# A DiT block on one Trainium2 core: the stream of the modulation rows and router weights moves from the last rank to the second

## The chip, the cores and the metric

The kernel is written in Bass for one core of a Trainium2 chip. The metric is the device time of one execution in microseconds (us). The engines are PE (TensorE: matmuls; PEld are its weight loads), DVE (VectorE), ACT (ScalarE), POOL (GpSimd) and SP (SyncE, which issues nearly all transfers, one after the other, in the order of its queue).

## What is computed

One layer over 1024 latent tokens of width 1024, with 256 context tokens ahead of them. Eight RWKV heads (a bidirectional recurrence) and four attention heads work on the same normalised input; their outputs, 512 columns each, are put side by side and go through one 1024x1024 output projection, scaled by a gate. Then each token is routed to 4 of 32 experts.

```python
p_lat = modulate(rmsnorm(x, norm1_g[l]), sh1, sc1) @ w_in[l]
y_rwkv, yc_rwkv = rwkv_mixer(p_lat[..., :RWKV_COLS], ...)
y_mla, yc_mla = mla_mixer(p_lat[..., RWKV_COLS:], ...)
x = x + gt1 * (jnp.concatenate([y_rwkv, y_mla], axis=-1) @ w_out[l])
h2 = modulate(rmsnorm(x, norm2_g[l]), sh2, sc2).reshape(B * T, D)
f = moe_ffn(h2, router_w[l], router_b[l], exp_w1[l], exp_b1[l], exp_w2[l], exp_b2[l])
x = x + gt2 * f.reshape(B, T, D)
return rmsnorm(x, final_norm_g)
```

The change touches the line with `w_out`: `gt1` (the gate) must be spread to all 128 partitions before it can be multiplied into `w_out`, and the scale and shift rows of the second modulation and the router's weights must be there before the logits of the router.

## The kernel before

The program has two phases. The first, some 1290 of 2711 us, is the mixer: projections, recurrence, attention, output projection and routing. The second, the 32 experts, is written in a fixed order and is not touched.

**The planner.** The mixer is not written in the order in which it runs. Each piece of work is a Python generator, a *stream*, which yields the engine, buffer or event that it wants next. A planner (`Weave`) keeps an estimated clock for each engine and lets, among the streams that its estimate holds ready for the engine that is free first, the one with the lowest *rank* record its next step; among equals the older one. `w.spawn(rank, generator)` starts a stream. The estimates only set the order of instructions on each engine's queue; on the chip an engine runs its queue in that order and waits by semaphores. All instructions of the mixer are recorded through one helper and show as line 972, so streams are told apart by shape, tile and position.

**The streams that matter here, with their ranks:**
- rank 0: the scan of the recurrence (chunk steps 0 to 19 one after the other; four context steps, then 16 latent ones), the solver of its chunk systems, `Mix.weights`; rank 1: the feeder of the scan's operands, routing of a block;
- rank 40 to 47: `Mix.rows(m)`, the second half of the output projection of token block m (of 8), which needs the recurrence's output (k = 0 to 3 of `w_out`), `early(m)`, and all of `w_out`;
- rank 52 to 59: `Mix.early(m)`, the first half, with attention's output (k = 4 to 7): x and y are fetched, 24 matmuls 128x512 in two halves of 12, two adds, one store to `x2`;
- rank 60: `Rwkv.readout(b)`, group normalisation and gate of the recurrence's output of block b, stored as `y`; rank 61: norm and logits of a block; rank 100 and 101: what hangs on the scan's outputs;
- rank 105, the last of all: `Mix.tables`, below.

The blocks go in the order 4, 3, 5, 2, 6, 1, 7, 0, as forward and backward scan meet in the middle.

**`Mix.tables`** starts when the fifth chunk system is solved. It loads the router's weights, adds and multiplies them with the modulation (8 matmuls 128x32, DVE), and spreads the gate, scale and shift rows over the partitions: six groups of four matmuls `kc,modc` 128x128, each followed by one ACT copy. Then it fires `placed`. **`Mix.weights`** waits for the end of attention and for `placed`. It loads `w_out` in eight slices of 512 KB into three stage buffers, slices 4 to 7 first; each is multiplied with the gate row (DVE for even, POOL for odd slices), copied as the high part by ACT, and the low part is taken by a DVE subtraction 128x1024, which frees the stage buffer. After four slices `early` may run, after eight `rows`.

**What holds readouts apart.** A readout needs the one buffer `SQ` twice: for the squares early in its chain, and for the transposed result that the store to `y` reads. So the next readout's squares wait until that store has landed. The chain of one readout is squares (ACT), sum and inverse root (15 or so small DVE operations), two POOL operations, a gate matmul, a DVE product, four transposes (PE), a copy (ACT), the store (SP).

**After the last block** a short routing part (`Route.lead`) turns the logits of block 0 into slots, gathers the first expert's rows from `h_d` by POOL, transposes them, and the experts start.

Of the kernel before, what the change touches and what calls it, by code (L numbers as in the profile page):

```python
# [651 lines left out]
class Route:  # L652
# [10 lines left out]
    def start(self, jobs):  # L663
        w, ex = self.w, self.ex
        ex.begin(jobs)
        self.J = jobs[0]
        w.spawn(50, self.early())
        w.spawn(50, self.loads())
        w.spawn(70, self.conversions())
# [307 lines left out]
class Weave:  # L977
# [75 lines left out]
    def run(self):  # L1053
        while self.live:
            self.settle()
            if not self.live:
                break
            start = {}
            for s in self.live:
                if isinstance(s["need"], str):  # L1060
                    e = s["need"]
                    s["from"] = s["ready"]
                    if s["room"]:
                        s["from"] = max(s["ready"], min((x[0] for x in s["room"].free), default=1e18))
                    start[e] = min(start.get(e, 1e18), max(s["from"], self.free[e]))
            if min(start.values(), default=1e18) > 1e17:
                raise RuntimeError("streams stuck: " + str([(s["rank"], s["gen"].__name__) for s in self.live]))
            e = min(start, key=start.get)
            t = start[e]
            cool = e == "pe" and self.clock.cool(t)  # L1070
            s = min((s for s in self.live if s["need"] == e and s["from"] <= t),
                    key=lambda s: (cool and not s["dense"], s["rank"], s["no"]))
            self.began, self.now, self.lag = t, t, self.LAG[e]
            if s["room"]:
                s["send"] = self.take(s["room"])
            self.resume(s)
            s["late"] = self.now + self.lag
            s["ready"] = self.now if s["on"] or e == "sp" else s["late"]
        return self.now
# [831 lines left out]
class Attention:  # L1911
# [19 lines left out]
    def split(self, hi, lo, src):  # L1931
# [4 lines left out]
        w.dve.tensor_sub(lo, src, hi.bitcast(F32))  # L1936

    def run(self, order, start):
        w, d = self.w, self.d
        yield start  # L1940
# [588 lines left out]
class Mix:  # L2529
# [23 lines left out]
    def start(self, order):  # L2553
        w = self.w
        w.spawn(0, self.weights())
        w.spawn(105, self.tables())
        w.spawn(61, self.more())
        for i, m in enumerate(order):
            w.spawn(52 + i, self.early(m))
            w.spawn(40 + i, self.rows(m))  # L2560
# [371 lines left out]
```

## Time and profile before

| | us |
|---|---|
| median of 3 runs | 2704.86 (2703.42 to 2709.39) |
| the profiled execution | 2712.86, span 2710.9 |
| attention's last store | 977.92 |
| loads of `w_out` issued | 1045.22 to 1083.12 |
| end of the scan's last matmuls | 1096.96 |
| first rows of the experts gathered (wait begins) | 1256.43 |
| experts | about 1290 to 2710 |

Times of events are counted from the start of the span. The stretch that the change concerns lies between 920 and 1290 us. The page's shares are averages over the whole span, of which the experts are more than half, and say little about it; the stretches of time and the chain of waits of that part say more. In the table of stretches a busy time next to the length of the stretch shows how full an engine is, and PEclk is the granted clock of TensorE as a share of its full speed.

### The profile page before, as it was taken

The numbers are of one execution on the slowest core, as the hardware profiler recorded it, in microseconds if no ns is written. First come the engines' busy times: TensorE is split into PE (matmuls) and PEld (weight loads), VectorE is DVE, ScalarE is ACT, GpSimd is POOL, SyncE is SP. The second block draws the span as 40 slices with busy tenths as digits, with TensorE's granted clock in tenths as the row PEclk, the third lists the DMA queues.
The fourth block names the chain that finished last, engine by engine and source line by source line (L and its number), as shares of the span: only waits on it lengthen the run. The fifth ranks groups of instructions, "written<-read, shape, count | busy, mean of one in ns | idle before, by whom it ended". The sixth has DMA issues, their size and how long they took to land.

```text
span 2710.9 us, 58835 instructions
## 1 busy us (share of the span) xinstructions
PE 2497.3 (92%) x23393; PEld 2185.5 (81%) x23428; DVE 2035.9 (75%) x4060; ACT 1634.4 (60%) x2633; POOL 491.3 (18%) x431
## 2 busy tenths in 40 slices
PE   5999995899999998796999999999999999999996
PEld 2666763677777787565999999999999999999995
DVE  6753865777775647676887887898988888898886
ACT  6233544656545434233686776787777777777785
POOL 1112443310111136310111110111101110111101
PEclk8899997889899888897999999999999999999997
DMA  6642445552323235655798897998999989999994
GB/s 249 236 182 59 117 111 121 121 165 81 120 87 103 71 115 152 220 204 191 277 333 280 305 330 277 322 337 295 333 312 328 335 309 325 317 329 330 315 331 162
DMA packets 240985, 622.52 MB, mean 230 GB/s; under 512 B 73080, under 2 KB 157176, under 8 KB 190400
## 3 DMA queue, kind: packets, MB, share of 16 engines
q1 hardware_dynamic: 229808, 581.96, 62.3%
q0 software_dynamic: 10896, 36.74, 5.6%
q8 instruction: 186, 3.05, 0.4%
q14 instruction: 95, 0.78, 0.1%
HBM read 544.09 MB, written 74.53 MB: 228 GB/s over the span
## 4 chain that ended last, share of the span: by engine, by line
PE 61%; DVE 24%; ACT 5%; issue 3%; DMA 3%; SPq 2%; POOL 1%; DVEq 0%; ACTq 0%; POOLq 0%
PE banks L972 28%; PE banks L384 15%; DVE at L357 9%; DVE at L972 8%; PE banks L395 8%; PE banks L388 7%; ACT at L972 2%; DVE at L410 2%; SPq L972 2%; PE banks L327 1%; DVE at L411 1%; DMA at<-y_d 1%; ACT at L349 1%; ACT at L409 1%; DVE at L412 1%
## 5 line engine op out<-in xcount | busy, mean ns | idle before, releaser
L972 PE MATMUL banks<-at,at 128*128 128x512 f32 (+8 forms) x3775 | 743.1, 354 | 78.1 <-ACT at L972 31.0
L384 PE MATMUL banks<-at,at 128*128 128x256 f32 (+11 forms) x5120 | 750.7, 299 | 0.8 <-DVE at L410 0.8
L357 DVE TENSOR_TENSOR at<-at,at 128x2048 bf16<-128x2048 f32 x316 | 721.4, 2283 | 0.0
L384 PEld LDWEIGHTS banks<-at,at 128*128 128x128 f32 x5120 | 685.0, 189 | 2.5 <-DVE at L410 1.2
L972 PEld LDWEIGHTS banks<-at,at 128*128 128x128 f32 (+3 forms) x3290 | 444.5, 186 | 223.6 <-issue 74.7
L349 ACT ACTIVATE at<-at 128x2048 fp32r<-128x2048 f32 x316 | 603.5, 1910 | 0.0
L972 ACT ACTIVATE at<-banks 128x512 f32<-128x512 f32 (+6 forms) x475 | 240.3, 524 | 320.8 <-PE banks L972 308.2
L388 PE MATMUL banks<-at,at 128*128 128x128 bf16 (+11 forms) x5120 | 382.5, 226 | 0.0
L972 DVE TENSOR_TENSOR at<-at,at 128x1024 fp32r<-128x1024 f32 (+26 forms) x364 | 261.7, 728 | 112.8 <-ACT at L972 103.1
L388 PEld LDWEIGHTS <-at 128*128 128x128 bf16 x5120 | 322.8, 96 | 21.8 <-issue 3.5
L972 ACT ACTIVATE at<-at 128x512 f32<-128x512 f32 (+9 forms) x259 | 175.1, 701 | 248.3 <-DVE at L972 100.9
L395 PE MATMUL banks<-at,at 128*128 128x128 f32 (+11 forms) x2048 | 273.0, 290 | 11.7 <-DVE at L419 11.3
L409 ACT ACTIVATE at<-banks,at 128x128 f32<-128x128 f32 (+11 forms) x512 | 183.4, 375 | 157.0 <-PE banks L388 121.6
L395 PEld LDWEIGHTS banks<-at,at 128*128 128x128 f32 x2048 | 256.5, 192 | 18.6 <-DVE at L419 18.0
L972 PE MATMUL banks<-at 64*64 64x64 f32 (+4 forms) x4880 | 230.9, 231 | 41.6 <-DVE at L972 23.4
L972 PEld LDWEIGHTS banks<-at 64*64 64x64 f32 (+3 forms) x4880 | 203.5, 142 | 72.0 <-DVE at L972 31.8
L972 PE MATMUL banks<-kc,at 128*128 128x128 f32 (+4 forms) x1136 | 179.1, 288 | 38.9 <-ACT at L972 19.7
L972 POOL TENSOR_TENSOR at<-at,at 128x512 f32<-128x512 f32 (+6 forms) x106 | 149.1, 1413 | 352.6 <-DVE at L972 317.7
L313 POOL DMA_INDIRECT at<-h_d,at x49 | 47.5, 969 | 897.3 <-DVE at L295 444.2
L972 POOL TENSOR_TENSOR at<-at 64x512 f32<-64x512 f32 (+3 forms) x94 | 123.8, 1324 | 428.8 <-ACT at L972 201.0
L972 PEld LDWEIGHTS banks<-kc,at 128*128 128x128 f32 (+2 forms) x1136 | 140.3, 169 | 72.2 <-issue 29.4
L458 POOL DMA_INDIRECT x_d<-at,at x50 | 122.8, 2456 | 327.8 <-ACT at L409 150.3
(158 smaller groups left out, 2127.3 us busy)
## 6 DMA issues: line engine op xcount, KB each, us to landing
at<-in_wexp SPq DMA_DIRECT2D x384, 1024.0 KB, 7.1
at<-in_mod_w SPq DMA_DIRECT2D x48, 512.0 KB, 6.2
at<-w_d SPq DMA_DIRECT2D x48, 384.0 KB, 4.0
at<-w_d SPq DMA_DIRECT2D x32, 512.0 KB, 5.1
at<-in_w_in SPq DMA_DIRECT2D x18, 512.0 KB, 3.5
x_d<-at SPq DMA_DIRECT2D x18, 512.0 KB, 3.0
at<-in_x SPq DMA_DIRECT2D x16, 512.0 KB, 5.5
w_d<-at SPq DMA_DIRECT2D x16, 512.0 KB, 4.3
```

Source lines behind the costliest of these rows:

```text
L313: nc.gpsimd.indirect_dma_start(out=xg[:R], out_offset=None, in_=self.d["h2"], in_offset=bass.IndirectOffsetOnAxis(ap=gi[:R, 0:1], axis=0))
L327: nc.tensor.transpose(p[:, k, :R], xg[:R, kk * 128:kk * 128 + 128], ident[:R, :R])
L349: self.nc.scalar.activation(wh, J["w", s], AF.Copy)
L357: self.nc.vector.tensor_sub(wl, J.pop(("w", s)), wh.bitcast(F32))
L384: nc.tensor.matmul(p[:, q, :2 * N], wh[:, k, q], X[:, k].rearrange("p s n -> p (s n)"), start=k == 0, stop=False, skip_group_check=True)
L388: nc.tensor.matmul(p[:, q, N:2 * N], wl[:, k, q], xt[:, k, 0, :, 1], start=False, stop=k == KT - 1, skip_group_check=True)
L395: nc.tensor.matmul(p[:, q, :N], w[:, k, q], J["H"][:, k], start=k == 0, stop=k == KT - 1, skip_group_check=True)
L409: nc.scalar.activation(u[:, q], p[:, q, N:2 * N], AF.Identity, bias=b)
L410: nc.vector.tensor_add(u, p[:, :, :N], u)
L411: nc.vector.tensor_scalar(u[:, 0], u[:, 0], 7.0, None, op0=OP.min)
L458: self.nc.gpsimd.indirect_dma_start(out=self.d["x2"], in_=J["yo", i][:R], in_offset=None, compute_op=OP.add, out_offset=bass.IndirectOffse ...
L972: return f(*args, **kw)
```

## The change

One number: the rank with which `Mix.tables` is started.

```diff
     def start(self, order):
         w = self.w
         w.spawn(0, self.weights())
-        w.spawn(105, self.tables())
+        w.spawn(1, self.tables())
         w.spawn(61, self.more())
```

No operation is added or removed; the planner records the mixer in another order. Three places follow.

SP around the loads of `w_out` before (at170 to at172 are the three stage buffers; `o_d` the scan's outputs, here those of scan step 16; at132 to at134 with `w_d` and `v_d` the feeder's loads for a scan step; at146, at149 a readout's; at173, at153 with `in_x` and `y_d` those of `early`):

```order
L972 DMA at141_228<-o_d_68 128x512
L972 DMA at170_257<-in_w_out 128x1024
L972 DMA at171_258<-in_w_out 128x1024
L972 DMA at172_259<-in_w_out 128x1024
L972 DMA at146_233<-v_d_60 128x4x64 x2
L972 DMA at149_236<-xg_d_61 128x128
L972 DMA y_d_67<-at147_234 128x4x128
L972 DMA at170_257<-in_w_out 128x1024
```

And now, where the `o_d` rows are those of scan step 12:

```order
L972 DMA at140_227<-o_d_68 128x512
L972 DMA at170_257<-in_w_out 128x1024
L972 DMA at171_258<-in_w_out 128x1024
L972 DMA at172_259<-in_w_out 128x1024
L972 DMA at141_228<-o_d_68 128x512
L972 DMA at133_220<-w_d_59 128x4x256 x2
L972 DMA at133_220<-v_d_60 64x256 x4
L972 DMA at170_257<-in_w_out 128x1024
L972 DMA at171_258<-in_w_out 128x1024
L972 DMA at172_259<-in_w_out 128x1024
L972 DMA at146_233<-v_d_60 128x4x64 x2
```

The loads stand four scan steps earlier; the fourth to sixth, which wait for a stage buffer to be freed, now stand ahead of the next readout's loads and of a feeder load for the scan. The conversions follow in scan steps 13 to 15 (before: 17 to 19).

PE at the end of the scan before (64x64 are matmuls of the recurrence; the last row with at133 is the scan's last set; at158 to at161 are the high parts of `w_out` slices 4 to 7, so the rows with them belong to `early`):

```order
L972 MATMUL banks_77<-at133_220 64x64 x16
L972 MATMUL banks_77<-at148_235,at149_236 128x512
L972 MATMUL banks_77<-at138_225,at135_222 64x64 x16
L972 MATMUL banks_77<-at133_220 64x64 x16
L972 MATMUL banks_77<-kc,at145_232 128x128 x4
L972 MATMUL banks_77<-kc,at140_227 128x128 x4
L972 MATMUL banks_77<-at133_220 64x64 x16
L972 MATMUL banks_77<-at158_245,at174_261 128x512
L972 MATMUL banks_77<-at159_246,at174_261 128x512
```

The same place now (at154 to at157 are the high parts of slices 0 to 3, so the rows with them belong to `rows`):

```order
L972 MATMUL banks_77<-at133_220 64x64 x16
L972 MATMUL banks_77<-at138_225,at135_222 64x64 x16
L972 LDWEIGHTS at180_9265
L972 MATMUL banks_77<-at162_249,at180_9265 128x512
...
L972 MATMUL banks_77<-at154_241,at178_8998 128x512
L972 MATMUL banks_77<-at155_242,at178_8998 128x512
L972 MATMUL banks_77<-at156_243,at178_8998 128x512
L972 MATMUL banks_77<-at157_244,at178_8998 128x512
L972 MATMUL banks_77<-at133_220 64x64 x16
```

Before, the first of the eight `early` blocks comes behind the scan's last matmuls. Now all eight stand ahead of them (blocks 4 and 3 after step 15, two more in each of steps 16, 17 and 18), and with them block 4 of `rows` with its logits, half of block 5 and four matmuls of block 2. Behind the scan stand blocks 5, 2, 3, 6 of `rows`, then 1, 7, 0.

SP at the end of the mixer before, from readout 0's store on (at147 is the buffer `SQ`, so `y_d<-at147` is a readout's store; a fetch of `x2_d` and `y_d` begins a block of `rows`):

```order
L972 DMA y_d_67<-at147_234 128x4x128
L972 DMA h2_d_70<-at134_221 128x1024
L972 DMA x2_d_69<-at132_219 128x1024
L972 DMA at235_9175<-in_wexp 128x2048
L972 DMA at236_9176<-in_wexp 128x2048
L972 DMA at134_221<-x2_d_69 128x1024
L972 DMA at134_221<-y_d_67 128x4x128
```

And now, from readout 7's store to the fetch of block 0:

```order
L972 DMA y_d_67<-at147_234 128x4x128
L972 DMA at173_260<-x2_d_69 128x1024
L972 DMA at153_240<-y_d_67 128x4x128
L972 DMA h2_d_70<-at134_221 128x1024
L972 DMA x2_d_69<-at173_260 128x1024
L972 DMA y_d_67<-at147_234 128x4x128
L972 DMA at132_219<-x2_d_69 128x1024
L972 DMA at132_219<-y_d_67 128x4x128
L972 DMA at235_9523<-in_wexp 128x2048
```

Each of the last three blocks of `rows` (1, 7, 0) is now fetched directly behind the store of its own readout, and the two expert weights come behind the last fetch, no longer ahead of it.

## Rows read from the trace of the kernel before

**Rows 1.** Stretches (start:end, length), busy us of PE, PEld, DVE, ACT, POOL; PEclk, DMA

```profile
978.00:1002.00 24.00, 23.84 (x417) 21.34 (x418) 11.03 (x19) 8.45 (x14) 8.47 (x12) 1.00 0.50 150
1002.00:1027.00 25.00, 21.99 (x243) 18.75 (x244) 12.85 (x33) 8.70 (x15) 13.46 (x14) 0.73 0.32 87
1050.00:1073.00 23.00, 16.70 (x308) 14.12 (x306) 19.12 (x25) 12.25 (x20) 20.46 (x13) 0.94 0.41 127
1073.00:1097.00 24.00, 13.57 (x211) 10.68 (x212) 21.25 (x21) 8.04 (x12) 17.52 (x12) 0.70 0.49 151
1175.00:1200.00 25.00, 23.89 (x133) 17.63 (x136) 21.37 (x68) 8.05 (x21) 5.79 (x6) 1.00 0.67 224
978.00:1097.00 119.00, 98.57 (x1513) 84.98 (x1514) 81.24 (x132) 43.79 (x70) 70.18 (x63) 0.87 0.48 145
1097.00:1264.00 167.00, 132.65 (x698) 94.23 (x710) 108.74 (x361) 44.98 (x123) 25.30 (x31) 0.89 0.60 206
1290.00:2710.00 1420.00, 1377.34 (x13403) 1335.82 (x13401) 1196.51 (x2386) 1058.29 (x1600) 180.29 (x107) 0.99 0.88 309
```

**Rows 2.** Timeline, the scan's end: start us, us, engine, line, operation, out<-in

```profile
986.10 1.05 SPq L972 DMA_DIRECT2D at<-o_d  x2
...
1045.22 1.38 SPq L972 DMA_DIRECT2D at<-in_w_out  x3
...
1060.25 9.60 SPq L972 DMA_DIRECT2D at<-in_w_out  x3
...
1085.34 0.33 SPq L972 DMA_DIRECT2D at<-in_x  x1
...
1095.81 1.15 PE L972 MATMUL banks<-at 128*64 128x64 f32 x32
```

**Rows 3.** The chain of waits after the scan: start us, us, what

```profile
1108.99 12.10 DMA at<-y_d
...
1175.07 7.56 PE banks L972 x32
...
1219.43 11.37 DMA at<-y_d
1230.88 0.64 ACT at L972
...
1256.43 6.35 DMA at<-h_d,at
```

**Rows 4.** Timeline of PE, logits of one half block

```profile
1150.82 0.98 PE L972 MATMUL banks<-at,at 128*128 128x32 f32 x8
...
1151.63 0.63 PE L972 MATMUL banks<-kc,at 128*128 128x128 f32 x4
```

**Rows 5.** Timeline of two readouts, from squares to store (in brackets the idle time before)

```profile
1023.62 0.63 ACT L972 ACTIVATE at<-at 128x512 f32<-128x512 f32 x1
...
1036.77 0.37 SPq L972 DMA_DIRECT2D y_d<-at  x1
...
1095.65 0.37 SPq L972 DMA_DIRECT2D y_d<-at  x1
...
1098.01 0.63 ACT L972 ACTIVATE at<-at 128x512 f32<-128x512 f32 x1 [0.87 <-DMA y_d<-at]
...
1120.32 1.15 SPq L972 DMA_DIRECT2D y_d<-at  x1
```

**Rows 6.** The page's transfers: issues, KB each, median us from issue to landing

```profile
at<-in_x SPq DMA_DIRECT2D x16, 512.0 KB, 5.5
```

**Rows 7.** Timeline of POOL and DVE, conversions of `w_out` slices

```profile
1054.91 3.24 POOL L972 TENSOR_TENSOR at<-at,at 128x1024 f32<-128x1024 f32 x1
...
1058.31 3.90 DVE L972 TENSOR_TENSOR at<-at,at 128x1024 bf16<-128x1024 f32 x2
...
1064.08 2.36 POOL L972 TENSOR_TENSOR at<-at,at 128x1024 f32<-128x1024 f32 x1 [0.75 <-DMA at<-in_w_out]
1064.28 5.23 DVE L972 TENSOR_TENSOR at<-at,at 128x1024 bf16<-128x1024 f32 x2
```

## The prediction

> **What bounds the kernel now.** I read the table of stretches first, then the chain of waits behind the scan, then the timeline around single waits. The experts keep PE busy for 1377.34 of 1420 us [rows 1] in an order that the change leaves alone, and they start when the last block is routed. So the question is only when the gather of the first expert's rows begins, 1256.43 us now [rows 3]; whatever moves that moves the end by as much. Ahead of it lie two parts. Up to 1096.96 us, where the scan's last matmuls end (1095.81 + 1.15) [rows 2], the scan's serial chain sets the pace and PE works beside it for 98.57 of 119 us [rows 1]; idle are 0.2 us of the slice 978 to 1002, 3.0 of 1002 to 1027, and 6.3 and 10.4 in the two from 1050 to 1097 [rows 1]. In those last two DVE is at 19.12 of 23 and 21.25 of 24 us, since the conversions of `w_out` fall there, and the scan's own DVE steps queue behind them. Behind the scan, 159.4 us (1256.4 − 1097.0) hold all sixteen half blocks of the output projection, and PE is nearly full while there is work for it (23.89 of 25 us) [rows 1].
>
> **What moves, term by term.** Nothing is removed. The tables end before the conversions need them, the loads of `w_out` follow the `o_d` loads that stand at 986.1 instead of 1045.2 us [rows 2], and so 59 us earlier the gate is open; work of PE that lay behind the scan is now in front of its end.
>
> *PE work moved ahead of the scan's end.* An `early` block is 24 matmuls; 32 of this size took 7.56 us, 0.236 each [rows 3], so a block is 5.67 us and eight are 45.4. With them go 24 + 12 + 4 = 40 matmuls of `rows`, 9.4 us, and the logits of one block, two halves of 0.98 + 0.63 us [rows 4], 3.2 us. Sum 58.0 us.
>
> *The scan's end.* Between 978 us and the scan's end PE then has 98.6 + 58.0 = 156.6 us of work, 37.6 more than the 119 us that it had. That is what it costs if PE never idles. But the conversions now lie in steps 13 to 15 and hold DVE there, while `early` is not yet allowed to fill the gap: I move the two slices' hole of 6.3 + 10.4 = 16.7 us with them. Against that stands the clock: in the slices at a granted clock of 0.73 and 0.70 lie 21.99 and 13.57 us of PE work [rows 1]; at 1.00 these would be 16.1 and 9.5, so 10.0 us less at the most. The denser stretches in the table have 1.00, the ones with holes have not; I take half, 5 us. The scan's end goes out by 37.6 + 16.7 − 5 = +49.3 us. Bounds: +27.6 (no hole, whole clock gain) and +54.3 (hole, no gain); with DVE stalls beyond these, see the third rival.
>
> *From the scan's end to the store of readout 1.* Behind the scan PE had 132.65 us [rows 1]; without the eight `early` blocks 87.2 remain, 10.9 for each of eight blocks with norm, logits, routing and readout. Blocks 5, 2, 3 and 6 are 43.6, less 16 matmuls (3.8) done before: 39.8. At the share of the fullest stretch here, 23.89 of 25 [rows 1], that is 41.6, and one fetch that nothing covers is 5.5 us [rows 6]: 47. Bounds 42 and 52.
>
> *The last readouts.* This is where the cover goes. Now readouts 1, 7 and 0 run while PE is busy with `early` and `rows`, and all their stores are out before their blocks are due. Afterwards nothing else is left to do, and each waits for the one before, since squares need the buffer that the store reads. From squares to store a readout took 13.15 us (1023.62 to 1036.77), from a store to the next squares 2.36 us (1095.65 to 1098.01), and beside block work 22.3 (1098.01 to 1120.32) [rows 5]. On PE's queue 12 matmuls of a block stand in the middle of each (2.8 us, and they wait for a fetch): I take 13.15 + 2.36 + 4 = 19.5 us a readout, between 15.5 and 24.7, the measured pairs. After readout 1 come two: 39.
>
> *The last block.* Store landing 2.4 us [rows 5], fetch 5.5 [rows 6]: 7.9 us, where before the last fetch took 11.37 [rows 3] behind two expert loads that now come after it. From its ACT copy to the gather it was 1256.43 − 1230.88 = 25.5 us [rows 3], a chain that the change leaves alone. 39 + 7.9 + 25.5 = 72.4; bounds 64 and 88.
>
> *Sum.* 49.3 + 47 + 72.4 = 168.7 us against 159.4 behind today's scan end: +9.3 us. The profiled execution took 2712.86 us, span 2710.9, and so goes to 2722; the median of the runs, 8 us lower, from 2704.86 to 2714. The change wins 159.4 − 119.4 = 40 us behind the scan and pays 49.3 in front of its end; it is a gain only if the scan's end moves by less than 40 us.
>
> **The rivals.** *Faster: PE is not as full in the scan as it looks.* Weight loads fill only 84.98 of the 119 us against 98.57 for matmuls [rows 1], and small sets whose ends overlap may make room for `early` without holding the scan. If the hole is filled as well and the clock stays at its higher level, 2.4 GHz, the scan's end moves by +27.6 us; the tail at 114 (42 + 72) gives 27.6 + 114 − 159.4 = −17.8, 2687 us; with a part of the hole, 2692. It decides from the 40 us above. For it speaks also that the 12.10 us fetch behind the expert weights at 1108.99 [rows 3] lay open and is gone in the new order; against it, that the slice 978 to 1002 has PE at 23.84 of 24 us. The Trainium skill (Perfetto Trace Analysis, section Identifying the Most-Contended Engine) says that busy time of matmuls is a bad measure of headroom and that weight-load busy time should be used. By it the stretch has 34 us of room in place of 20, and the whole change would be a gain. The trace so far doesn't settle it: in the experts both measures stand above 0.94.
>
> *No difference.* The serial readouts run at 15.5 us, as PE has nothing else: the tail is 8 us shorter, the sum +1.3, 2706 us.
>
> *Slower still: SP and DVE stall the scan.* The fourth to sixth load of `w_out` wait on SP until a stage buffer is free; before, SP stood 9.60 us over such three loads (1060.25) and the first of them came 15.0 us after the first load (1045.22) [rows 2]. Now a feeder load of the scan and a readout's loads stand right behind. If the feeder's lead of about a step doesn't cover it, the scan waits up to 15 us: +24.3, 2729 us. The conversions may also get slower: the two subtractions without POOL beside them took 3.90 us, two with a POOL product beside them 5.23 [rows 7], 0.67 us more each, some 5 us over eight. The Trainium skill (SBUF, section Who interferes with whom) gives the reason: a DVE operation with two SBUF inputs and a GpSimd operation that reads SBUF share one port pair, an exclusive lock. The rows agree with it, and it adds nothing to the sum, as the same pairs met before.
>
> That the change does nothing is out: the queues of the engines differ from scan step 12 on, as the pieces above show.
>
> **How the numbers follow.** Forecast 0.48 (own range 2706 to 2724: 0.34 slower, 0.14 within); faster 0.24 (0.20, and 0.04 within); no difference 0.14 (0.10 within, 0.02 on either side); slower still 0.14. A measurement of this kernel can't tell 0.2 %, 5.4 us, from no change. So faster 0.22, same 0.28, slower 0.50. Range: from the middle of the faster rival to the far end of the slower one, 2690 to 2734.
>
> **What would show it.** In the profile after, the first loads of `w_out` at some 987 us; PE over 0.9 busy from about 1040 us to a scan end near 1146 us; then the stores of readouts 1, 7 and 0 some 19 us apart with PE half idle between them; a gather near 1266 us; the experts as long as before. I am wrong if the scan ends before 1130 us, if the last readouts are done under block work, or if `w_d` and `v_d` loads land late and the scan stands still in steps 13 to 15.

## The result and the profile after

The change makes the kernel slower. The median of 11 runs is 2733.38 us (2723.27 to 2739.32) against 2709.39 us (2698.13 to 2721.07) for 11 runs of the kernel before; the ratio is 1.0093, with a 95% interval of 1.0076 to 1.0109, that is +24.0 us (20.6 to 29.5 from the ends of the interval). The prediction said +9.3 us with the right sign and about the right two halves; the time lies in its range, near the far end.

The profiled execution took 2738.96 us, with a span of 2737.1. The table of stretches of the kernel after (columns as in [rows 1]) has the stretches of [rows 1] from 1002 to 1097, then the longer road to the scan's end, what lies behind it, and the experts:

```profile
1002.00:1027.00 25.00, 19.69 (x268) 17.74 (x265) 21.79 (x22) 10.65 (x14) 16.66 (x11) 0.74 0.70 217
1027.00:1050.00 23.00, 16.36 (x168) 12.28 (x168) 18.51 (x30) 6.25 (x9) 15.92 (x15) 0.70 0.53 173
1050.00:1073.00 23.00, 22.26 (x223) 16.60 (x223) 10.50 (x25) 6.10 (x10) 5.67 (x5) 1.00 0.63 181
1073.00:1097.00 24.00, 23.61 (x281) 18.39 (x284) 13.96 (x31) 5.73 (x10) 8.52 (x9) 1.00 0.68 215
1097.00:1125.00 28.00, 27.20 (x269) 20.05 (x271) 16.31 (x35) 7.79 (x15) 9.18 (x8) 1.00 0.46 144
1125.00:1160.00 35.00, 31.35 (x281) 23.75 (x284) 18.91 (x41) 9.55 (x18) 10.31 (x13) 0.85 0.49 160
...
1160.00:1210.00 50.00, 42.30 (x238) 30.61 (x242) 37.91 (x140) 16.17 (x52) 8.40 (x8) 0.83 0.48 165
1210.00:1260.00 50.00, 31.25 (x138) 21.89 (x139) 33.01 (x113) 14.12 (x38) 11.89 (x11) 0.74 0.44 144
...
1315.00:2736.00 1421.00, 1377.13 (x13405) 1335.86 (x13404) 1197.38 (x2386) 1058.36 (x1600) 176.73 (x107) 0.99 0.88 309
```

Three things are to be seen. The experts take what they took, 1377.13 us of PE against 1377.34 in [rows 1], so all of the loss is ahead of them. From 1050 to 1125 us PE is full (22.26 of 23, 23.61 of 24, 27.20 of 28) where it had holes before; the conversions, which keep DVE and POOL busy, now lie in the two slices from 1002 to 1050. And from 1210 to 1260 us PE works 31.25 of 50 us. The last 71.6 us up to the gather, in the kernel before:

```profile
1184.80:1256.40 71.60, 58.54 (x326) 42.92 (x328) 52.06 (x193) 25.48 (x74) 6.80 (x10) 0.87 0.56 194
```

and in the kernel after, where PE does 15.0 us less in the same length and its granted clock is lower:

```profile
1210.30:1281.90 71.60, 43.57 (x203) 30.56 (x205) 43.90 (x155) 17.80 (x52) 12.15 (x12) 0.73 0.44 150
```

The timeline of the kernel after, at the places of [rows 2] and [rows 5] (start us, us, engine, line, operation): the ACT operation with which scan step 12 and then step 15 starts, loads of `w_out`, the scan's last matmuls, and the last three stores of a readout, of blocks 1, 7 and 0.

```profile
981.64 0.60 ACT L972 ACTIVATE at<-banks 128x512 f32<-128x512 f32 x1
...
999.04 1.72 SPq L972 DMA_DIRECT2D at<-in_w_out  x3
...
1010.28 0.35 SPq L972 DMA_DIRECT2D at<-in_w_out  x1
...
1030.77 0.58 ACT L972 ACTIVATE at<-banks 128x512 f32<-128x512 f32 x1
...
1157.92 1.54 PE L972 MATMUL banks<-at 128*64 128x64 f32 x32
...
1210.34 0.38 SPq L972 DMA_DIRECT2D y_d<-at  x1
...
1230.11 0.43 SPq L972 DMA_DIRECT2D y_d<-at  x1
...
1251.08 0.39 SPq L972 DMA_DIRECT2D y_d<-at  x1
```

The scan's last matmuls end at 1159.46 instead of 1096.96 us, and the last three readouts store 19.8 and 21.0 us apart. The last store goes out 30.9 us ahead of the gather; before it was 44.7 us ahead, and the row of the kernel before is:

```profile
1211.73 0.37 SPq L972 DMA_DIRECT2D y_d<-at  x1
```

The chain of waits of the kernel after (start us, us, what) at the end, to be laid beside [rows 3]:

```profile
1213.71 4.67 DMA at<-y_d
...
1259.40 0.62 ACT at L972
...
1281.93 6.56 DMA at<-h_d,at
```

The gather is waited for from 1281.93 instead of 1256.43 us. The one fetch that shows takes 4.67 us, where fetches of 12.10 and 11.37 us stood before: the change did remove those, and lost more elsewhere. What took their place is in the shares of that chain from the scan's end to the gather, some 162 us before and 125 after. Before:

```profile
by line: PE banks L972 45.1%; DVE at L972 25.1%; DMA at<-y_d 14.5%; ACT at L972 5.3%; issue 4.5%; DMA at<-h_d,at 3.9%; DMA x_d<-at 2.1%; SPq L972 1.8%; DVE lg L972 0.5%; DVEq L972 0.1%; ACTq L972 0.1%
```

After:

```profile
by line: DVE at L972 46.1%; PE banks L972 32.5%; ACT at L972 9.4%; DMA at<-h_d,at 5.2%; issue 5.1%; DMA at<-y_d 3.7%; DVE lg L972 0.9%; SPq L972 0.5%; DVEq L972 0.1%; ACTq L972 0.1%
```

Fetches fall from 14.5% to 3.7%, and DVE rises from 25.1% to 46.1%, that is from some 41 to 58 us: the small operations of norms, routing and readouts, which ran beside block work before, now are links of the chain.

**One execution is not one instruction's time.** Step 12 of the scan, in which the loads of `w_out` now go out, starts at 974.52 us in the profile of before and at 981.64 in that of after. Over the 17 profiles of this study it starts between 969.1 and 982.1 us, in no order that goes with the change: the two kernels of the study that keep `tables` at its old rank and move a readout's rank have 970.8 and 970.7, the change measured again 970.6. So those 7.1 us are for the most part spread between executions (what the tables' own work may have of them stands further down), and from here on the stretch from step 12 to the gather is compared, cut at the scan's end (the end of the DVE copy 64x512 of step 19, 1.2 to 1.7 us ahead of the last matmuls' end). "Idle" is the length less PE's busy time. All in us, one profiled execution each.

| kernel | step 12 to scan's end | PE idle | scan's end to gather | PE idle | step 12 to gather | scan's end to last readout store | last store to gather |
|---|---|---|---|---|---|---|---|
| before | 120.8 | 20.4 | 161.2 | 27.8 | 281.9 | 116.5 | 44.7 |
| before, again (e9) | 119.6 | 19.7 | 160.9 | 27.7 | 280.5 | 116.0 | 44.9 |
| after | 176.6 | 19.0 | 123.7 | 36.1 | 300.3 | 92.8 | 30.9 |
| after, again (e8) | 176.8 | 16.5 | 125.7 | 35.1 | 302.5 | 94.8 | 30.9 |

The two pairs differ by 18.4 and 22.0 us, 20 in the mean; the rest of the 24.0 us of the medians was not located. Single profiles carry an error of their own: that of e10 below is 8.2 us short of the median of its kernel (2710.17 and 2718.39 us), so a few us between two stretches say nothing.

### The profile page after: what moved, and what is told of

It is laid out like the page before. It is cut to its first block, busy times and chain, and to the rows that moved or that the text cites. A ratio compares the mean times of both kernels' runs of the same rounds, so it can differ in the third digit from the quotient of the medians.

```text
span 2737.1 us, 58807 instructions
## 1 busy us (share of the span) xinstructions
PE 2519.3 (92%) x23388; PEld 2200.8 (80%) x23428; DVE 2034.8 (74%) x4060; ACT 1633.8 (60%) x2633; POOL 488.3 (18%) x431
## 4 chain that ended last, share of the span: by engine, by line
PE 62%; DVE 25%; ACT 5%; issue 3%; DMA 3%; SPq 2%; POOL 1%; DVEq 0%; ACTq 0%; POOLq 0%
PE banks L972 29%; PE banks L384 15%; DVE at L972 9%; DVE at L357 9%; PE banks L395 8%; PE banks L388 7%; ACT at L972 2%; DVE at L410 2%; SPq L972 1%; PE banks L327 1%; DVE at L411 1%; ACT at L409 1%; DVE at L412 1%; ACT at L349 1%; PE banks L452 1%
## 5 line engine op out<-in xcount | busy, mean ns | idle before, releaser
L972 PE MATMUL banks<-at,at 128*128 128x512 f32 (+8 forms) x3754 | 752.1, 357 | 74.4 <-POOL at L972 25.7
L395 PE MATMUL banks<-at,at 128*128 128x128 f32 (+11 forms) x2048 | 273.1, 290 | 11.9 <-DVE at L419 11.5
L972 PE MATMUL banks<-at 64*64 64x64 f32 (+4 forms) x4896 | 242.4, 236 | 34.6 <-DVE at L972 19.0
L395 PEld LDWEIGHTS banks<-at,at 128*128 128x128 f32 x2048 | 256.6, 192 | 18.9 <-DVE at L419 18.2
L972 PEld LDWEIGHTS banks<-at 64*64 64x64 f32 (+3 forms) x4896 | 213.9, 147 | 69.3 <-issue 30.8
```

What stands on the lines that cost most here:

```text
L395: nc.tensor.matmul(p[:, q, :N], w[:, k, q], J["H"][:, k], start=k == 0, stop=k == KT - 1, skip_group_check=True)
L972: return f(*args, **kw)
```

## The experiments

Unless another kernel is named, each is an edit of the kernel after. "Stretch" is step 12 to gather. The ratios are to the kernel before, with their 95% intervals.

### e8 and e9: the change and the kernel before, again

The first has no edit, the second is the kernel before.

> The changed kernel itself, for a second profiled execution. If the 7.1 us by which scan step 12 came later in the first one is the early tables' cost, it is there again (step 12 at 980 us or more); if it is the spread between executions, step 12 lies between 969 and 982 as in the other four variants with the same order up to there, and from step 12 to the gather it takes about 300 us again. Ratio 1.008 to 1.011.

> The kernel before once more, for a second profiled execution. From scan step 12 to the gather the first one took 281.9 us, the changed kernel 300.3 and 302.5. If the first was typical, 279 to 285 us again; if the 24 to 28 us between the medians are all in this stretch, about 275 us.

Measured: 1.0118 [1.0093, 1.0144] and 1.0011 [0.9988, 1.0034]. The table of stretches of e8, up to the scan's end and from there to the gather:

```profile
971.00:1148.00 177.00, 160.48 (x1768) 127.13 (x1778) 106.89 (x190) 51.60 (x85) 74.13 (x67) 0.88 0.55 173
1148.00:1273.00 125.00, 89.97 (x473) 64.52 (x476) 82.78 (x296) 35.22 (x105) 20.91 (x20) 0.75 0.44 152
```

and the same of the kernel before, in its first profile:

```profile
974.50:1095.30 120.80, 100.37 (x1550) 86.59 (x1551) 81.10 (x132) 44.22 (x71) 68.89 (x59) 0.87 0.47 142
1095.30:1256.40 161.10, 133.26 (x731) 94.63 (x740) 108.73 (x355) 46.68 (x126) 24.26 (x28) 0.91 0.58 201
```

The loss repeats. PE does 60.1 us more ahead of the scan's end (160.48 − 100.37) at nearly the same granted clock, and the stretch grows by 56.2 (177.00 − 120.80): work that goes in front of the scan's end delays that end about one for one, with the idle time ahead of it much as it was. Behind the scan's end PE does only 43.3 us less (133.26 − 89.97), at a granted clock of 0.75 instead of 0.91. So of the 20.1 us by which the two stretches together grow (302.00 − 281.90), PE is busy for 16.8 us more, with no more matmuls to do, and idle for 3.3 us more. In the first pair it is 11.5 and 6.9 us. An emptier end shows as slower matmuls as well as idle time.

### e3: the readouts ahead of the blocks

The likeliest place of the loss was the end, where three readouts follow one another with little beside them. Here a readout goes ahead of all block work.

```diff
-                    w.spawn(60, self.readout(bl[d], O))
+                    w.spawn(39, self.readout(bl[d], O))
```

> The changed kernel, with readouts at rank 39, ahead of rows and early, so that readouts 1, 7 and 0 stand among the blocks and not behind them. Theory A: the scan ends as late as in the changed kernel (about 1160 us), but the last three stores no longer lie 20 us apart at the end; the last rows block follows the one before it at PE's pace and the gather comes 15 to 25 us sooner than in the changed kernel: ratio to before 1.000 to 1.004. Theory B: as the changed kernel, 1.008 to 1.010.

Measured: 0.9998 [0.9975, 1.0021], 2704.7 us against 2708.37: the loss is gone. Its two stretches, cut at the scan's end:

```profile
969.00:1144.00 175.00, 151.47 (x1768) 120.27 (x1775) 106.66 (x201) 52.78 (x88) 76.81 (x71) 0.93 0.57 178
1144.00:1245.00 101.00, 82.22 (x472) 62.45 (x478) 76.50 (x283) 33.95 (x103) 14.93 (x19) 0.82 0.54 185
```

and its last three stores of a readout:

```profile
1147.96 0.37 SPq L972 DMA_DIRECT2D y_d<-at  x1
...
1186.79 0.38 SPq L972 DMA_DIRECT2D y_d<-at  x1
...
1212.01 0.37 SPq L972 DMA_DIRECT2D y_d<-at  x1
```

The scan ends as late as in the change (175.1 us after step 12 by the exact marks). All of the recovery is behind it: 101.2 us to the gather instead of 123.7, PE idle 19.0 instead of 36.1, the last store 25.0 us earlier counted from the scan's end (67.8 against 92.8). The readouts stand further apart now (38.8 and 25.2 us), but block work runs between them.

### e5: the readout's result in a buffer of its own

This takes away the buffer that ties a readout to the one before: the result that is stored no longer lies in the one buffer `SQ`, but stays in `C`, of which there are two, until the store has landed.

```diff
-        w.put(self.C, t)
-        yt = yield self.SQ
...
-        w.act.activation(flat(yt), p, AF.Copy)
+        w.act.activation(f, p, AF.Copy)
...
-        w.put(self.SQ, yt, 2000)
+        w.put(self.C, t, 2000)
```

> The changed kernel, with a readout's transposed result copied into its own buffer (C, of which there are two) in place of SQ, so that the next readout's squares no longer wait for the store. Theory A (the readouts, one after the other at the end, are the loss): in the changed kernel the last stores are 19.8 and 21.0 us apart; if SQ is what holds them, they come 10 to 15 us apart, the gather 8 to 15 us sooner than in the changed kernel, ratio to before 1.003 to 1.006. If it is their rank behind rows that holds them and not the buffer, 1.006 to 1.010. Theory C (the scan's end, 55 us later, is the whole loss): 1.008 to 1.010.

Measured: 1.0037 [1.0012, 1.0062], 2717.89 against 2705.9 us; stretch 284.5. Its stretches up to and behind the scan's end:

```profile
976.00:1151.00 175.00, 157.11 (x1793) 123.89 (x1799) 109.87 (x205) 54.80 (x91) 78.85 (x72) 0.93 0.58 178
1151.00:1261.00 110.00, 78.73 (x448) 58.35 (x454) 79.74 (x284) 32.25 (x100) 13.79 (x17) 0.79 0.48 168
```

More than half of the loss comes back by the medians, 15.8 of the 18.4 us by the first pair of stretches, and again behind the scan's end (109.9 us to the gather). The scan's end is 174.6 us after step 12, nearly as in the change. But not in the way expected. The stores were to come 10 to 15 us apart; the one of readout 1 is out early, at 1161.36 us, and the last two are as far apart as in the change:

```profile
1207.97 0.37 SPq L972 DMA_DIRECT2D y_d<-at  x1
...
1230.05 0.39 SPq L972 DMA_DIRECT2D y_d<-at  x1
```

The edit took one readout out of the end. That the buffer holds the last two apart, it does not show; their 22.1 us have another cause (see the last readouts below).

### e13: the kernel before with the readouts last

If a serial end is enough for the loss, then it must cost as much without any early `w_out`. The edit is of the kernel before, with `tables` at rank 105:

```diff
-                    w.spawn(60, self.readout(bl[d], O))
+                    w.spawn(110, self.readout(bl[d], O))
```

> The kernel before (tables at rank 105) with readouts at rank 110, behind all block work: readouts 6, 1, 7 and 0 come one after the other at the end, each followed by its own rows block, as in the changed kernel, without early tables. If the serial end is what costs the 20 us, it costs them here too: the last stores about 20 us apart with nothing under them, the gather 15 to 30 us later than before, ratio 1.006 to 1.012. If the loss in the changed kernel comes from what was moved ahead of the scan's end, 0.999 to 1.004.

Measured: 1.0063 [1.004, 1.0087], 2727.82 against 2708.11 us; stretch 300.4, as long as with the change. Up to and behind the scan's end:

```profile
971.00:1084.00 113.00, 93.32 (x1521) 81.54 (x1520) 67.58 (x101) 40.87 (x65) 56.91 (x51) 0.88 0.44 135
1084.00:1271.00 187.00, 148.95 (x770) 105.24 (x768) 120.92 (x385) 49.39 (x132) 34.19 (x37) 0.85 0.54 183
```

and the last three stores:

```profile
1195.12 0.38 SPq L972 DMA_DIRECT2D y_d<-at  x1
...
1220.37 0.37 SPq L972 DMA_DIRECT2D y_d<-at  x1
...
1241.86 0.37 SPq L972 DMA_DIRECT2D y_d<-at  x1
```

The scan ends earlier than before (113.2 us after step 12), and yet the gather is late: the last stores are 25.3 and 21.5 us apart (19.8 and 21.0 in the change), 38.2 us of PE behind the scan's end are idle, and from the last store to the gather it takes 29.2 us, near the 30.9 of the change. Readouts at the end, without early tables, make the stretch as long as the change does, and cost more than half of its loss by the medians. The length alone is no fingerprint, though: e1, e4 and e6 below come to 1.0075 to 1.0098 with other ends.

### e14: is it the granted clock?

In the change PE has a granted clock of 0.78 behind the scan, against 0.91 before (0.73 and 0.87 in the last 71.6 us). So the loss could be matmuls that are slower. Here 16 more matmuls 128x512 stand ahead of the products of blocks 1, 7 and 0.

```diff
+        if m in (1, 7, 0):
+            p = yield "pe", self.B
+            for k in range(16):
+                w.pe.matmul(p, self.woh[k % 4][:, 0:128], self.woh[k % 4][:, 512:1024], start=True, stop=True)
+            w.put(self.B, p)
```

> The changed kernel with 16 extra matmuls 128x512 on PE ahead of each of the last three rows blocks (their result is not used), so that PE is not half idle between the last readouts. If the lower clock of that stretch (0.70 to 0.75) is on the path, the real matmuls get shorter there and the gather comes no later or up to 5 us sooner: ratio 1.006 to 1.010 to before. If the readouts alone set the pace, the extra matmuls cost what they stick out, 0 to 9 us: 1.009 to 1.014, with a granted clock above 0.85 there and the stores as far apart as before.

Measured: 1.0099 [1.0071, 1.0128]; stretch 303.2, against 300.3 and 302.5 for the change. The stretches from 1210 us on in the change (to the gather), then the same in e14:

```profile
1210.00:1250.00 40.00, 26.68 (x109) 18.06 (x111) 25.37 (x86) 9.02 (x27) 11.64 (x10) 0.74 0.35 109
1250.00:1282.00 32.00, 17.19 (x99) 12.80 (x97) 18.86 (x72) 9.08 (x25) 0.58 (x3) 0.72 0.57 203
```

```profile
1210.00:1250.00 40.00, 31.04 (x132) 22.83 (x133) 24.12 (x83) 8.81 (x26) 11.61 (x10) 0.83 0.31 97
1250.00:1284.00 34.00, 20.46 (x114) 15.61 (x112) 18.54 (x71) 9.09 (x25) 0.50 (x2) 0.78 0.53 186
```

The costliest groups of PE there (line, engine, operation, out<-in, shape, count | busy us, mean ns | idle before), in the change:

```profile
L972 PE MATMUL banks<-at,at 128*128 128x512 f32 x52 | 21.3, 575 | 8.2 <-ACT at L972 6.1 <-DVE at L972 2.0
```

and in e14, the real ones and below them the added ones:

```profile
L972 PE MATMUL banks<-at,at 128*128 128x512 f32 x52 | 16.0, 469 | 2.0 <-ACT at L972 1.2 <-DVE at L972 0.8
L972 PE MATMUL banks<-at 128*128 128x512 f32 x46 | 14.5, 479 | 0.0
```

The clock rose to 0.83 and 0.78, less than I had expected, and the 52 real matmuls took 16.0 instead of 21.3 us. The end did not move, and the ratio lies in both expected ranges, so the run does not choose between them. Its chain of waits shows why: the first and the third set of added matmuls stand on it, 6.0 and 5.6 us long, in these two pieces:

```profile
1212.71 10.94 PE banks L972 x38
...
1258.04 9.16 PE banks L972 x32
```

PE holds 48.0% of that chain from 1208 us on, against 35.9% from 1210 us on in the change. The real matmuls got shorter and the added ones took the time: the stores are now 15.8 and 26.6 us apart, and from the last one to the gather it takes 33.3 us instead of 30.9. What the lower clock costs in the change is thus not shown; as PE holds a third of the chain there, it need not be nothing. Waits for small operations and slower matmuls come together when the end has no cover, and no run here parts them.

### e2: the conversions back behind step 15

Theory: the conversions, by holding DVE in steps 13 to 15, cost scan time. New events are fired at each scan step's end, and `w_out` is loaded only after step 15.

```diff
+            w.fire(self.stepped[j])
...
         yield self.placed
+        yield self.rwkv.stepped[15]
```

> The changed kernel, with the loads and conversions of w_out held until scan step 15 is recorded, so that they fall in steps 15 and 16 and some three early blocks and one rows block stand ahead of the scan's end instead of eight and one and a half. Theory A: the scan ends about 7 + 30 us later than before, the tail is shorter by the 25 us of work moved, ratio 1.002 to 1.007, between before and the change. Theory B: conversions are no cheaper there, ratio 1.008 or more.

Measured: 1.0035 [1.0018, 1.0053], stretch 283.9. The scan's end comes 156.4 us after step 12, the rest takes 127.5, with PE idle 24.7. That is the ratio and the scan's end of theory A (35.6 us later than before), while the tail is shorter by 33.7 us, not 25. Fewer blocks get ahead of the scan's end, and more of them are left to run beside the last readouts. That is the same trade at another point; it does not show that the conversions' place as such costs anything (e15).

### e1 and e10: the blocks held back

In e1 `early` waits for the scan's end, in e10 for step 17 only.

```diff
         yield self.early_ready
+        yield self.rwkv.end
```

> The changed kernel, with the eight early blocks held until the scan's last step is recorded; tables and conversions stay early. Theory A (the projection's matmuls in PE's queue delay the scan by some 50 us and are paid back only in part behind it): the scan ends 7 to 15 us later than before instead of 62.5, all sixteen half blocks run behind it under which the readouts are hidden, the gather comes 0 to 10 us later than before, ratio to before 1.000 to 1.004. Theory B (tables and conversions beside scan steps 12 to 15 are the harm, the blocks fill holes): the scan ends 25 us or more later than before, ratio 1.008 or more.

> The changed kernel, with the early blocks held until scan step 17 is recorded (in the first holding run they waited for step 19): blocks 4 and 3 stand ahead of the scan's last set, and their fetches go out before the expert weights do. If that first run lost 8 to 20 us because fetches and expert weights left SP together behind the scan, this one loses nothing: 278 to 286 us from step 12 to the gather, ratio 0.998 to 1.003. If early conversions cost something of their own, 1.006 or more.

Measured: e1 1.0081 [1.0055, 1.0107], stretch 294.0; e10 1.004 [1.0019, 1.0062], stretch 280.6. I expected e1 to be near the kernel before, and it is not. The scan's end is back (125.4 us after step 12), but behind it come 168.6 us instead of 161.2. The blocks' fetches are issued only when the scan has ended, and on the chain of waits three of them lie open (4.73, 6.22 and 8.31 us), 19.3 us together; in the kernel before it were two, 23.5 us [rows 3]. So open fetches don't explain its loss, which stays open in part. e10's stretch is as short as before, as expected, while its median is 10.9 us over it and its ratio lies between the two expected ranges: its profiled execution (2710.17 us) was the second fastest of eight. It settles nothing.

### e4: `early` behind everything

```diff
-            w.spawn(52 + i, self.early(m))
+            w.spawn(102 + i, self.early(m))
```

> The changed kernel, with early at ranks 102 to 109, so that an early block is recorded only where nothing else is ready: two blocks and one rows block ahead of the scan's last step, the rest behind. Theory A: the scan ends 7 + 20 us later than before, the tail holds what is left with the readouts covered, ratio 0.998 to 1.004. Theory B: 1.008 or more.

Measured: 1.0075 [1.005, 1.0099], stretch 290.2; a miss. The scan's end comes after 140.5 us, and the last readout stores 75.3 us behind it, early. But then 74.4 us pass to the gather, and PE idles 34.9 us behind the scan: two first halves are fetched only behind the last readout's store (at 1198.30 and 1207.81 us), and the second halves of their blocks behind them. There is still an end without cover, with other work in it.

### e6 and e7: is rank 39 a gain of its own?

e6 is the kernel before with the edit of e3; e7 is the change with the edits of e3 and e5 together.

> The kernel before (tables at rank 105) with readouts at rank 39. Theory A: the last readouts were hidden under block work there, so that their rank buys nothing: ratio 0.998 to 1.003. If the rank of the readouts is a gain of its own, apart from the change: 0.996 or less, and then the run of the changed kernel with that rank says less about the change.

> The changed kernel with readouts at rank 39 and the result in their own buffer. Theory A: the readouts of blocks 7 and 0 come one behind the other right after the scan's last outputs, all block work is behind them and PE is full to the last block: 5 to 10 us less than with rank 39 alone, ratio 0.996 to 0.999. Theory C: no better than rank 39 alone, 0.999 to 1.002.

Measured: e6 1.0098 [1.0071, 1.0125], 2728.81 against 2705.9 us; e7 0.9997 [0.9976, 1.0019], stretch 276.5. e6 surprised: the same edit that takes the loss away from the change costs as much in the kernel before. With the readouts done early, two loads of expert weights, which are issued once all readouts are done, go out at 1188.39 us ahead of four blocks' fetches. But the two fetches that lie open on its chain, 10.23 and 8.01 us, are no longer than the two of the kernel before (12.10 and 11.37 us [rows 3]), so they are not the loss. 80.9 us pass from the last store to the gather; behind the scan PE is idle for 38.3 us, against 27.8, at a granted clock of 0.85 against 0.91. Which wait makes this end longer was not found. So the recovery in e3 is not a gain that rank 39 brings everywhere: it mends the end that the change made, and costs time where the end was covered. e7 is no better than e3 (theory C): the buffer adds nothing that shows once the readouts are out of the end.

### e11, e12 and e15: mixtures

All three are the change with the edit of e3. e11 adds that of e2; e12 adds to e11 that the conversions get the rank 102; e15 adds that rank alone:

```diff
-            w.spawn(0, self.weight(k, x))
+            w.spawn(102, self.weight(k, x))
```

> The changed kernel with conversions held to scan step 15 and readouts at rank 39: five early blocks and one rows block ahead of the scan's last step, the readouts of 7 and 0 with block work behind them. Theory A (what is moved ahead of the scan's end is given back one for one; gain or loss is made by what idles behind it): the scan ends 35 to 45 us later than before, the tail is 40 to 48 shorter, 272 to 280 us in all, ratio 0.994 to 1.001.

> As the run before, and the conversions at rank 102 in place of 0, so that they are recorded where the scan leaves DVE and POOL free. If the conversions' hold on DVE is what keeps PE idle in the scan (16 to 25 us in all runs), idle time ahead of the scan's end falls by 5 to 10 us, ratio 0.990 to 0.998; if not, as the run before.

> The changed kernel with readouts at rank 39 and conversions at rank 102, early as in the change: conversions where the scan leaves DVE free, readouts under block work. If the conversions' place is worth anything, 268 to 275 us from step 12 to the gather, ratio 0.993 to 0.998; if PE's work is all that counts, as with rank 39 alone, 274 to 280, 0.998 to 1.002.

Measured: e11 1.0042 [1.0018, 1.0066], e12 1.0025 [1.0, 1.0049], e15 1.0009 [0.9995, 1.0023]; stretches 285.4, 282.0 and 277.0. None beats the kernel before, and e11 misses its range. It has 55.6 us from the last store to the gather, as more block work is left over: two edits that each help don't add up. In e12 the idle time ahead of the scan's end does not fall (24.8 us, 25.0 in e11). Putting the conversions last in e15 moves nothing against e3 (277.0 and 276.3): that their place costs time by itself shows in none of these runs.

## Why the prediction was right and wrong

**The mechanism held, but for one wait.** The prediction said that the change moves PE work in front of the scan's end, pays for it there, and can't get as much back behind it because the last readouts lose their cover. The kernels e3, e5 and e13 show the second half: relieve the end and the loss goes (wholly or by more than half) with the scan's end where it was; put the readouts last in the kernel before and a stretch of the change's length comes out, 300.4 us. The wait that it had wrong is the one between the last readouts.

**The last readouts and the last block: the time right, one wait wrong.** Predicted 39 us for two readouts and 72.4 from readout 1's store to the gather; measured 40.7 (1251.08 − 1210.34) and 71.6 (1281.93 − 1210.34). Within it the last fetch and copy took 8.3 us for 7.9, and the last block's chain 22.5 for 25.5. But the prediction has each readout wait for the store of the one before, as its squares need the buffer. In the trace of the kernel after the squares of readouts 7 and 0 (second and fourth row) start right behind an ACT operation of the routing, which had waited for DVE:

```profile
1213.56 0.30 ACT L972 ACTIVATE at<-at,at 128x4 f32<-128x4 f32 x1 [3.25 <-DVE at L972]
...
1213.85 0.61 ACT L972 ACTIVATE at<-at 128x512 f32<-128x512 f32 x1
...
1236.08 0.30 ACT L972 ACTIVATE at<-at,at 128x4 f32<-128x4 f32 x1 [4.00 <-DVE at L972]
...
1236.38 0.61 ACT L972 ACTIVATE at<-at 128x512 f32<-128x512 f32 x1
```

They come 3.5 and 6.3 us behind the store, where 2.36 us had been enough for a landing [rows 5]: what held them is the norm and routing of other blocks on DVE and ACT, ahead of them in the queues; by that measure the buffer was free before. In e8 they stand in the same place, behind waits of 3.96 and 4.00 us. e5, without the shared buffer, agrees with 22.1 us between its last stores. From squares to store it took 16.3 and 14.7 us, where the prediction had 17.15. That these add up to 40.7 us, near the 39 predicted, is luck.

**Scan's end to readout 1's store: somewhat low.** Predicted 47 us (42 to 52), measured 50.9 (1210.34 − 1159.46). PE worked 42.30 of the 50 us from 1160 to 1210, at a granted clock of 0.83, where I had let it work at the share of the fullest stretch, whose clock is 1.00 [rows 1].

**The scan's end: the mis-sized term.** Predicted +49.3 us, measured +55.8 by the marks of the table (176.6 − 120.8), and 57.2 in the second pair. The sum made PE busy for 53.0 us more (58.0 of work less 5 by the clock) and idle for 3.7 us less (16.7 for 20.4). Measured: busy for 57.3 us more (157.65 − 100.37) and idle for 1.4 us less (19.0 for 20.4). So 4.3 us fall on the step "I take half, 5 us", the gain by the clock, and some 2.3 on the hole, which filled less than I thought. The mean granted clock up to the scan's end is 0.89, after 0.87 before, and the work went in almost whole. The slices from 1050 to 1125 have 1.00, as I had hoped; but the conversions took their holes to 1002 to 1050, where the clock is 0.74 and 0.70, and the last slice has 0.85. The bound without the gain, +54.3, was nearly the measured value.

**A term put at nothing: the tables' own work.** The prediction says of the tables only that they end before the conversions need them. Their `kc,modc` matmuls from step 12 to the scan's end, before:

```profile
L972 PE MATMUL banks<-kc,modc 128*128 128x128 f32 x32 | 4.4, 281 | 0.0
```

and after:

```profile
L972 PE MATMUL banks<-kc,modc 128*128 128x128 f32 x8 | 1.2, 288 | 0.0
```

The other 24, some 3.2 us, now stand ahead of step 12, where PE has no room (busy for 45.88 of the 47 us from 935 to 982), and outside the stretches compared here. Step 12 starts at 975.3 us in the mean of the 13 profiles with early tables, and at 972.8 in that of the four without. These 2.5 us are within the spread, so this cost is likely, but not shown.

These terms explain 6.5 + 3.9 − 0.8 = 9.6 us over the forecast, 18.9 in all, against 18.4 in the first pair of profiles (the marks differ by a few tenths). The medians say 24.0; the tables' own work may be some 2 to 3 of the last 4 to 6 us, and for the rest I have no place in the trace.

**The rivals.** *Faster* fell at its first condition. The scan's end moved by more than the 40 us from which it decides, and the tail gained 37.5 (161.2 − 123.7), not 45. The Trainium skill (Perfetto Trace Analysis, section Identifying the Most-Contended Engine) would judge TensorE's headroom by MFU and by weight-load busy time. By the second there were 34 us of room here, by the busy time of matmuls 20.4; measured, 58 us of work cost 55.8, as much as if there had been hardly any. In this stretch the busy time of matmuls missed by less. *No difference* needed readouts of 15.5 us; they took 19.8 and 21.0. *Slower still* gave 2729 us, near the measured median, for a reason that the trace refutes: steps 12 to 15, in which SP and DVE were to stall the scan, took 49.1 us (1030.77 − 981.64) against 47.9 before, where steps 12 and 15 start with these rows:

```profile
974.52 0.60 ACT L972 ACTIVATE at<-banks 128x512 f32<-128x512 f32 x1 [0.72 <-PE banks L972]
...
1022.42 1.17 ACT L972 ACTIVATE at<-banks 128x512 f32<-128x512 f32 x2
```

The scan's end moves out in steps 15 to 19, 127.5 us against 72.9, where the eight `early` blocks stand in front of the scan's matmuls on PE's queue. The conversions did not get slower either: their eight subtractions took 13.1 us (12.9 in e8), after 18.9 before (16.0 in e9). And [rows 7] were read wrongly for their price: beside the pair that took 3.90 us POOL worked too, with operations 128x512 from 1058.10 to 1063.34 us, so they don't set a pair without POOL against one with it. A time that comes out near a rival's number is no evidence for it.

**What was to be seen in the profile.** The first loads of `w_out` came at 999 us, not 987 (7 of the 12 are the later step 12); PE was over 0.95 busy from 1050 to 1125 and 0.90 from there on; the stores 20 us apart and PE at 0.63 of 1210 to 1260 are as said; the scan's end and the gather were later than said by 13 and 16 us, of which 7.1 are the later step 12.

## What to carry to other kernels

A piece of work that is moved ahead of a serial chain on the same engine costs its whole length there as soon as that engine is full, so its gain must be sought behind the chain, in the waits that it ends there (here 58 us of work delayed the chain by 56 and 57 us). Work that can run at any time is worth most as cover for a serial end: before it is moved forward, see what else the last steps have beside them, and what each of them waits for. And compare stretches between two marks of the same execution, since the same instruction stood up to 13 us apart in executions of kernels that did the same up to there.

## What the runs showed of the hardware

- With no more matmuls to do from step 12 to the gather, PE was busy for 250.45 us in e8 and 233.63 in the kernel before; behind the scan its granted clock was 0.75 and 0.91. Idle time is not all that an emptier stretch costs.
- In e14 added matmuls with no use raised the granted clock from 0.74 to 0.83 and from 0.72 to 0.78, and the real matmuls 128x512 took 308 instead of 410 ns each (16.0 and 21.3 us over 52). The end did not come sooner; two of the three sets of added ones stood on the chain of waits themselves.
- The fetch of a block's `y` that showed on the chain took 4.67 us in the change, with no expert weights ahead of it. Behind three loads of expert weights it took 12.10 us in the kernel before and 10.23 in e6, behind two 11.37 and 8.01.
